# A decoder trunk on one core: state space work and attention probabilities placed otherwise, the gated spatial branch transposed by VectorE and transfers

## The chip, the cores and the metric

The kernel runs on one core of one Trainium2 chip. The metric is the device time of one execution in microseconds (us); several runs are made, and their median counts. A profile of one execution gives the start and the duration of every instruction on the core's engines: TensorE (PE, with its weight loads as PEld), VectorE (DVE), ScalarE (ACT), GpSimd (POOL), and SyncE (SP), whose queue issues nearly all transfers.

## The reference

Two layers, each of three blocks on h, which is 256 tokens by 1024 channels: half a SwiGLU block, a hybrid mixer, half a SwiGLU block, each between a norm before and a norm after. The mixer makes one input projection and sends its columns into three branches:

```python
y_a = moba_attention(q, k, v)            # 8 heads x 128, causal; one block of 256 keys here
xbc = silu(causal_conv(xbc)); dt = softplus(dt_raw + dt_bias)
y_s = ssd_scan(xs, dt, a, bm, cm) + d_skip[:, None] * xs      # 16 heads x 64, chunks of 128
y_s = rms_norm(y_s * silu(z), ssm_norm_g)
u  = gelu(u)
vg = layer_norm(gelu(vg), sgu_ln_g, sgu_ln_b)
sv = einsum('gij,bcjgd->bcigd', tril(sgu_w), vg) + sgu_b      # 8 groups, chunks of 128 tokens
y_c = u * sv
merged = gate0 * (y_a @ p_attn) + gate1 * (y_s @ p_ssm) + gate2 * (y_c @ p_sgu)
out = merged @ w_out
```

All inputs and weights are float32.

## The kernel before

**Tiles.** Tokens stand in two tiles t of 128. A weight block is 128 x 1024 and comes from memory by one transfer (`load`, L160) into a ring of six `raw` tiles. `split` (L180, L181) makes two parts of it, `whi` by ScalarE and `wlo` by VectorE, in rings of eleven. A product takes three matmuls: high by high, low weight by high input, high weight by low input (`unit`, L213 to L215). One call of `unit` is two such triples, six matmuls of 512 columns; a block takes two calls, one for each tile t.

**What sets the order.** Every engine works through its instructions in the order in which the program issues them. The program walks through the matmuls (`gemm`) and after each call of `unit` calls `pump`, which lets `tick` advance the waiting tasks by 1.3 for a call of six matmuls. A task is a generator: what stands between two `yield`s is issued at once, and the number yielded says how long it rests, in units that are near a microsecond of TensorE's work. The table `W` holds these rests. After `tick`, `pump` splits one more weight block, if one was used up. `finish` drives a task to its end at once.

**Layouts.** A product's input is needed with channels on the partitions. Two ways lead there. `to_parts` (L312 and on) transposes 128 x 128 pieces on TensorE into PSUM and makes the high and low part from there. `turn` and `land` go another way: VectorE transposes 32 x 32 squares in place (L277), four transfers write the tile to device memory in another arrangement (L280), and one transfer reads it back (L285); the weights that meet such an input have their rows rearranged on the host (`_woven`). Before the change the SwiGLU hidden tiles, the keys, the probabilities `sc` and the state space result `y` go by `turn`; the spatial branch's `u` goes by `to_parts`.

**The mixer's order.** xbc, z, q, k and v projections with convolution and state space work beside them (`ssd`: for tile t and group g two calls of `weights`, then products `yd`); the first branch product (`br` with `ysh`, `ysl`); projection vg, with attention's tile 1 beside it (`attention`: scores, exponentials, `turn`, `land`, then value products `pv`, L837); the gate and branch product of attention; projection u, with the gelus and the layer norm of vg (`spatial_norm`, L866 to L872); the last gate projection, eight blocks, with the spatial products `sv` (L882, `sgu`) beside it; the last branch product (`br` with `ych`, `ycl`); the output projection.

In `sgu` the tile t = 0 has its two pairs of spatial products, a rest of 9.1 and its transposes; only then comes t = 1. `spatial_norm` issues its work for t = 1 when the u projection has been issued, ahead of `sgu`.

Of the kernel before, what the change touches and what calls it, by code (L numbers as in the profile page):

```python
# [9 lines left out]
F32 = mybir.dt.float32  # L10
BF16 = mybir.dt.bfloat16
F32R = mybir.dt.float32r
AF = mybir.ActivationFunctionType
ALU = mybir.AluOpType
# [30 lines left out]
ACC, TR = 5, 3  # L45


W = {'gw': 6.5, 'tr': 0, 'parts': 0, 'sq': 1.3, 'lead': 3.9, 'sq2': 5.2, 'hh': 5.2, 'x0': 0.65, 'cv': 5.2, 'cs': 6.5, 'xs': 0, 'dt1': 2.6, 'dt2': 0, 'dt3': 5.2, 'cb': 2.6, 'w1': 2.6, 'w2': 6.5, 'ys': 3.9, 'qk': 3.9, 'vv': 0, 'qs': 0, 'ex': 0, 'p1': 10.4, 'p2': 0, 'p3': 3.9, 'ge': 0, 'ln': 10.4, 'sv': 0, 'yc': 9.1, 'mg': 3.9, 'pv': 11.7, 'out': 7.8, 'in': 9.1}


@with_exitstack
def trunk(ctx, tc, a):
# [435 lines left out]
    def mixer(l, x, r2, nxt):  # L488
# [189 lines left out]
        def ssd(ysx, rs):  # L678
# [13 lines left out]
            def scaled(t):  # L692

                y[t] = b4(f"y{t}")
                G.tensor_tensor(h3(y[t]), h3(xs[t]), hpar[:, l, 2, :, None].to_broadcast([P, SH, SP]),
                                op=ALU.mult)
                xdt[t] = xs[t]
                V.tensor_tensor(h3(xdt[t]), h3(xs[t]),
                                st["dt"][:, t * SH:(t + 1) * SH, None].to_broadcast([P, SH, SP]), op=ALU.mult)
# [19 lines left out]
            for t in range(NT):  # L719
                for g in range(SG):  # L720
                    weights(t, 2 * g)
                    if g == 0:
                        scaled(t)
                    yield W["w1"]
                    weights(t, 2 * g + 1)
                    if t == 0:

                        pst = tr("state")
                        T.matmul(pst, bc["b"][:, g * P:(g + 1) * P], xw[:, 512 * g:512 * g + 512],
                                 start=True, stop=True)  # L730
                        A.copy(state[:, 512 * g:512 * g + 512], pst)
                    yield W["w2"]
                    c = slice(512 * g, 512 * g + 512)
                    py = tr("yd")
                    for q in (2 * g, 2 * g + 1):
                        for j in range(4):
                            hh = q * 4 + j
                            T.matmul(py[:, (hh - 8 * g) * SP:(hh - 8 * g + 1) * SP], ws[t, q][:, j, :],
                                     xdt[t][:, hh * SP:(hh + 1) * SP], start=True, stop=True)
                        ws.pop((t, q))  # L740
                    V.tensor_tensor(y[t][:, c], py, y[t][:, c], op=ALU.add)
                    if t == 1:
                        po = tr("yo")
                        T.matmul(po, cT(g, 1), state[:, c], start=True, stop=True)
                        tmp = b2("yo")
                        V.tensor_tensor(h3(tmp, 8), h3(po, 8),
                                        st["eac"][:, 8 * g:8 * g + 8, None].to_broadcast([P, 8, SP]), op=ALU.mult)
                        V.tensor_tensor(y[t][:, c], y[t][:, c], tmp, op=ALU.add)
                    V.tensor_tensor(y[t][:, c], y[t][:, c], zs[t][:, c], op=ALU.mult)
                rs[t] = rsqrt([sumsq(y[t], "sy")], "rs", 1.0 / D)  # L750
                yt[t] = spawn(turned(t, y[t], pl[:, G_SSM:G_SSM + 8]), wait=1.3)


        qk = {}
# [26 lines left out]
        def attention(yax, free):  # L781
            for t in range(NT):
# [36 lines left out]
                for g in range(2):  # L819
# [2 lines left out]
                                    rden[:, None, 4 * g:4 * g + 4, None].to_broadcast([P, 4 * m, 4, 32]), op=ALU.mult)  # L822
                    rd[g] = turn(sc[g], m)
                    yield 1.3
                yield W["out"]
                for g in range(2):
                    land(sc[g].rearrange("p (m e) -> p m e", m=m), rd[g])
                yield W["pv"]
# [13 lines left out]

        uu, vg = {}, {}

        def gelu_evac(store, name, c, ps):

            for t in range(NT):
                if t not in store:
                    store[t] = b4(f"{name}{t}")
                p1 = ps[t]  # L850
                xx = b2("gx")
                A.activation(xx, p1, AF.Copy, scale=r2[t])
                x2 = b2("gx2")
                A.activation(x2, p1, AF.Square, scale=r2[t])
                V.scalar_tensor_tensor(x2, x2, 1.0 / A_GELU, xx, op0=ALU.add, op1=ALU.mult)
                A.activation(x2, x2, AF.Tanh, scale=C_GELU * A_GELU)
                V.scalar_tensor_tensor(store[t][:, 512 * c:512 * c + 512], x2, 1.0, xx, op0=ALU.add, op1=ALU.mult)
                yield W["ge"]

# [15 lines left out]
        def sgu(ycx):  # L875
            ws = wsp[l][0]
            for t in range(NT):
                for q in range(2):
                    ps = tr("sv")
                    for j in range(4):  # L880
                        g = 4 * q + j
                        T.matmul(ps[:, j * P:(j + 1) * P], ws[:, g, :], vg[t][:, g * P:(g + 1) * P],  # L882
                                 start=True, stop=True)
                    for j in range(4):
                        g = 4 * q + j
                        o = uu[t][:, g * P:(g + 1) * P]
                        V.scalar_tensor_tensor(o, ps[:, j * P:(j + 1) * P], pl[:, G_SB + g:G_SB + g + 1], o,
                                               op0=ALU.add, op1=ALU.mult)
                    yield W["sv"]
                yield W["yc"]  # L890
                yield from to_parts(uu[t], *ycx.new(t), scale=0.5)


        merged = {}
# [27 lines left out]
                yield W["mg"]  # L922
                yield from to_parts(merged[t], *then.new(t))

        def branch(bx, rs, need, first=False, then=None):
            store = {}
            es = []
            for c in range(2):
                [ps] = project("gate")
                es.append(spawn(gate_evac(store, c, ps, rs)))  # L930
            finish(*need)
            finish(*es)
            slots, dst = accs("br")
            ready, out = set(), {}

            def on_done(key, t):
                ready.add((key, t))
                if t not in out:
                    out[t] = spawn(merge(t, slots, ready, store, first, then))

            gemm(chunk(0) + chunk(1), bx.h, bx.l, dst, tail=8 if then is not None else 0, on_done=on_done)
            return out

# [27 lines left out]
        b1 = branch(yax, None, [att, *b0.values()])  # L971
        gw = spawn(spatial_weights(l))
        finish(*gl)
        gl = [spawn(gelu_evac(uu, "u", 0, project("u")[0]))]
        finish(gw)
        sn = spawn(spatial_norm())
        gl.append(spawn(gelu_evac(uu, "u", 1, project("u")[0])))
        finish(*gl, sn)
        sg = spawn(sgu(ycx))
        b2_ = branch(ycx, None, [sg, *b1.values()], then=mx)  # L980
        ready = set()

        def mh(k, t):
# [145 lines left out]
def _arrays(i):  # L1129
# [3 lines left out]
    q, k, v, z, xbc, dt, u, vg, g0, g1, g2 = (w[:, :, s:e] for s, e in zip(cut[:-1], cut[1:]))  # L1133
    k = _woven(k, 512)
    weave = lambda m: _woven(np.swapaxes(m, 1, 2), 512).swapaxes(1, 2)
    order = [xbc, z, q, k, v, g1, weave(f["p_ssm"]), vg, g0, f["p_attn"], u, g2, f["p_sgu"], f["w_out"]]
    mix = [_chunks(m).reshape(L, -1, P, 1024) for m in order]
    col = lambda m: m.reshape(L, -1, P).transpose(0, 2, 1)
    par = np.concatenate(
# [39 lines left out]
```

## Time and profile before

| | |
|---|---|
| runs | 1492.39, 1489.04, 1489.55 us; median 1489.55 |
| the profiled execution's own time | 1490.6 us |
| its span, first to last instruction | 1488.8 us |
| mean granted TensorE clock | 0.992 of 2.4 GHz |
| weight blocks | 495, of 512 KB |

TensorE's matmuls overlap: one of 512 columns is shown with 0.39 us, and the next starts 0.23 us after it. An idle time in square brackets ends a row of the timeline, with what ended it. In the windows, PEclk is the granted clock as a share of 2.4 GHz; 0.50 is 1.2 GHz. Times of a layer are those from the span's start; layer 1's mixer comes some 736 us after layer 0's.

### The profile page before, as it was taken

What the parts mean: (1) busy time and instruction counts of PE and PEld (TensorE: products, weight loads), DVE (VectorE), ACT (ScalarE), POOL (GpSimd) and SP (SyncE); (2) the same over time, 40 slices, a digit from 0 to 9 for tenths busy, and PEclk for the clock granted to TensorE, in tenths of its full rate; (3) what the DMA queues carried; (4) which work ended last, traced back from release to release, by engine and by line L of the source; (5) the groups of instructions that cost most, each with busy time, mean ns of one, the idle gap of its engine ahead of it and who ended that gap; (6) DMA issues with size and microseconds to landing.
All of it is one profiled execution on the core that took longest, in us unless ns stands there. A gap on an engine that the chain in (4) does not pass through costs nothing. (4 is left out here: it accounts for less than half of the span.)

```text
span 1488.8 us, 18560 instructions
## 1 busy us (share of the span) xinstructions
PE 1461.8 (98%) x6706; PEld 1208.7 (81%) x6706; DVE 970.3 (65%) x1188; ACT 767.7 (52%) x1051; POOL 55.0 (4%) x98
## 2 busy tenths in 40 slices
PE   9999999989989999999999999999899899999998
PEld 7888888778878888888888888888788788888886
DVE  6766477767666857666486564876776677676652
ACT  6544367455454537444364443765463635464541
POOL 0000020000000000000000000200000000000000
PEclk9999999999999999999999999999999999999999
DMA  8978555577567445878568874656774765477760
GB/s 293 332 228 263 185 191 177 161 209 224 198 213 224 172 156 197 282 243 255 154 205 268 253 251 128 221 171 187 227 230 150 230 211 169 132 261 249 262 199 28
DMA packets 151003, 312.23 MB, mean 210 GB/s; under 512 B 35456, under 2 KB 76544, under 8 KB 150912
## 3 DMA queue, kind: packets, MB, share of 16 engines
q1 hardware_dynamic: 150336, 310.73, 64.3%
q8 instruction: 52, 0.85, 0.2%
q10 hardware_dynamic: 576, 0.33, 0.1%
q14 instruction: 39, 0.32, 0.1%
HBM read 288.98 MB, written 22.02 MB: 209 GB/s over the span
## 5 line engine op out<-in xcount | busy, mean ns | idle before, releaser
L181 DVE TENSOR_TENSOR wlo<-raw,whi 128x1024 fp32r<-128x1024 f32 x495 | 593.9, 1222 | 325.9 <-ACT whi L180 323.5
L180 ACT CAST whi<-raw 128x1024 fp32r<-128x1024 f32 x495 | 511.7, 1051 | 394.8 <-PE gu L215 162.9
L213 PE MATMUL gu<-whi,xh 128*128 128x512 f32 x704 | 276.1, 392 | 1.7 <-ACT xh L328 1.3
L214 PE MATMUL gu<-wlo,xh 128*128 128x512 f32 x704 | 274.9, 391 | 0.0
L215 PE MATMUL gu<-whi,xl 128*128 128x512 f32 x704 | 274.8, 390 | 0.0
L213 PEld LDWEIGHTS gu<-whi,xh 128*128 128x128 f32 x704 | 132.6, 188 | 30.2 <-ACT xh L328 1.7
L214 PEld LDWEIGHTS gu<-wlo,xh 128*128 128x128 f32 x704 | 132.6, 188 | 28.0 <-DVE wlo L169 0.9
L215 PEld LDWEIGHTS gu<-whi,xl 128*128 128x128 f32 x704 | 132.6, 188 | 28.1 <-DVE xl L329 0.4
L213 PE MATMUL dn<-whi,hTh 128*128 128x512 f32 x352 | 137.5, 391 | 0.0
L215 PE MATMUL dn<-whi,hTl 128*128 128x512 f32 x352 | 137.0, 389 | 0.0
L214 PE MATMUL dn<-wlo,hTh 128*128 128x512 f32 x352 | 136.9, 389 | 0.0
L215 PEld LDWEIGHTS dn<-whi,hTl 128*128 128x128 f32 x352 | 66.1, 188 | 13.9
L213 PE MATMUL gate<-whi,xh 128*128 128x512 f32 x192 | 77.1, 402 | 0.0
L214 PEld LDWEIGHTS dn<-wlo,hTh 128*128 128x128 f32 x352 | 66.1, 188 | 13.6
L213 PEld LDWEIGHTS dn<-whi,hTh 128*128 128x128 f32 x352 | 66.1, 188 | 13.3
L215 PE MATMUL gate<-whi,xl 128*128 128x512 f32 x192 | 75.4, 393 | 0.0
L214 PE MATMUL gate<-wlo,xh 128*128 128x512 f32 x192 | 75.2, 392 | 0.0
L328 ACT CAST xh<-xg 128x512 fp32r<-128x512 f32 (+1 forms) x25 | 15.1, 603 | 63.0 <-DVE xg L326 63.0
L713 ACT ACTIVATE ssw<-ssw,nacs 128x128 f32<-128x128 f32 x64 | 20.5, 391 | 50.8 <-DVE ssw L709 50.8
L215 PEld LDWEIGHTS gate<-whi,xl 128*128 128x128 f32 x192 | 36.3, 189 | 7.8
L214 PEld LDWEIGHTS gate<-wlo,xh 128*128 128x128 f32 x192 | 36.4, 190 | 6.9
L213 PEld LDWEIGHTS gate<-whi,xh 128*128 128x128 f32 x192 | 36.4, 190 | 6.8
(239 smaller groups left out, 2231.3 us busy)
## 6 DMA issues: line engine op xcount, KB each, us to landing
raw<-in_mix SPq DMA_DIRECT2D x232, 512.0 KB, 4.5
raw<-in_gu SPq DMA_DIRECT2D x175, 512.0 KB, 4.9
raw<-in_dn SPq DMA_DIRECT2D x88, 512.0 KB, 4.5
turn<-hh SPq DMA_DIRECT2D x160, 64.0 KB, 1.8
hh<-turn SPq DMA_DIRECT2D x40, 256.0 KB, 5.2
row_ffn_post_g<-in_ffn_post_g SPq DMA_DIRECT2D x4, 512.0 KB, 5.7
turnw<-qtok SPq DMA_DIRECT2D x32, 64.0 KB, 2.2
qT<-turnw SPq DMA_DIRECT2D x4, 512.0 KB, 5.9
```

The costliest lines, as they stand in the source:

```text
L180: A.copy(hi, w)
L181: V.tensor_tensor(lo, w, hi.bitcast(F32), op=ALU.subtract)
L213: T.matmul(o, xh(k, t), hi[:, off:off + n], start=first, stop=False)
L214: T.matmul(o, xh(k, t), lo[:, off:off + n], start=False, stop=False)
L215: T.matmul(o, xl(k, t), hi[:, off:off + n], start=False, stop=last)
L328: A.copy(o_h, xg)
L713: A.activation(w[:, j, :], w[:, j, :], AF.Exp, bias=st["nacs"][:, c:c + 1])
```

## The change

Five things change. The scaling of the state space input of tile 1 (`scaled(1)`: one GpSimd and one VectorE operation) is issued with group 1 of tile 0 instead of group 0 of tile 1, and the transposing of y of tile 0 starts after a rest of 6.5 instead of 1.3. The probabilities are read back after a rest of 3.9 instead of 7.8, and the value products follow after 13.0 instead of 11.7. `sgu` issues the spatial products of both tiles one after the other. The gated result u is no longer transposed by TensorE: a new task `turned_sum` for each tile transposes it in place, writes it, reads it back and makes the two parts; the host rearranges the rows of `p_sgu`. The last branch product waits for this task tile by tile (`late`), and the factor 0.5 moves from the transposes into the gelu of u.

```diff
@@ -45,7 +45,7 @@
 ACC, TR = 5, 3
 
 
-W = {'gw': 6.5, 'tr': 0, 'parts': 0, 'sq': 1.3, 'lead': 3.9, 'sq2': 5.2, 'hh': 5.2, 'x0': 0.65, 'cv': 5.2, 'cs': 6.5, 'xs': 0, 'dt1': 2.6, 'dt2': 0, 'dt3': 5.2, 'cb': 2.6, 'w1': 2.6, 'w2': 6.5, 'ys': 3.9, 'qk': 3.9, 'vv': 0, 'qs': 0, 'ex': 0, 'p1': 10.4, 'p2': 0, 'p3': 3.9, 'ge': 0, 'ln': 10.4, 'sv': 0, 'yc': 9.1, 'mg': 3.9, 'pv': 11.7, 'out': 7.8, 'in': 9.1}
+W = {'gw': 6.5, 'tr': 0, 'parts': 0, 'sq': 1.3, 'lead': 3.9, 'sq2': 5.2, 'hh': 5.2, 'x0': 0.65, 'cv': 5.2, 'cs': 6.5, 'xs': 0, 'dt1': 2.6, 'dt2': 0, 'dt3': 5.2, 'cb': 2.6, 'w1': 2.6, 'w2': 6.5, 'ys': 3.9, 'qk': 3.9, 'vv': 0, 'qs': 0, 'ex': 0, 'p1': 10.4, 'p2': 0, 'p3': 3.9, 'ge': 0, 'ln': 10.4, 'sv': 0, 'yc': 9.1, 'mg': 3.9, 'so': 3.9, 'pv': 13.0, 'uo': 5.2, 'out': 7.8, 'in': 9.1}
 
 
 @with_exitstack
@@ -719,8 +719,8 @@
             for t in range(NT):
                 for g in range(SG):
                     weights(t, 2 * g)
-                    if g == 0:
-                        scaled(t)
+                    if t == 0:
+                        scaled(g)
                     yield W["w1"]
                     weights(t, 2 * g + 1)
                     if t == 0:
@@ -748,7 +748,7 @@
                         V.tensor_tensor(y[t][:, c], y[t][:, c], tmp, op=ALU.add)
                     V.tensor_tensor(y[t][:, c], y[t][:, c], zs[t][:, c], op=ALU.mult)
                 rs[t] = rsqrt([sumsq(y[t], "sy")], "rs", 1.0 / D)
-                yt[t] = spawn(turned(t, y[t], pl[:, G_SSM:G_SSM + 8]), wait=1.3)
+                yt[t] = spawn(turned(t, y[t], pl[:, G_SSM:G_SSM + 8]), wait=1.3 if t else 6.5)
 
 
         qk = {}
@@ -822,7 +822,7 @@
                                     rden[:, None, 4 * g:4 * g + 4, None].to_broadcast([P, 4 * m, 4, 32]), op=ALU.mult)
                     rd[g] = turn(sc[g], m)
                     yield 1.3
-                yield W["out"]
+                yield W["so"]
                 for g in range(2):
                     land(sc[g].rearrange("p (m e) -> p m e", m=m), rd[g])
                 yield W["pv"]
@@ -842,18 +842,18 @@
 
         uu, vg = {}, {}
 
-        def gelu_evac(store, name, c, ps):
+        def gelu_evac(store, name, c, ps, half=1):
 
             for t in range(NT):
                 if t not in store:
                     store[t] = b4(f"{name}{t}")
                 p1 = ps[t]
                 xx = b2("gx")
-                A.activation(xx, p1, AF.Copy, scale=r2[t])
+                A.activation(xx, p1, AF.Copy, scale=r2[t] if half == 1 else halfr[t])
                 x2 = b2("gx2")
                 A.activation(x2, p1, AF.Square, scale=r2[t])
                 V.scalar_tensor_tensor(x2, x2, 1.0 / A_GELU, xx, op0=ALU.add, op1=ALU.mult)
-                A.activation(x2, x2, AF.Tanh, scale=C_GELU * A_GELU)
+                A.activation(x2, x2, AF.Tanh, scale=half * C_GELU * A_GELU)
                 V.scalar_tensor_tensor(store[t][:, 512 * c:512 * c + 512], x2, 1.0, xx, op0=ALU.add, op1=ALU.mult)
                 yield W["ge"]
 
@@ -887,8 +887,23 @@
                         V.scalar_tensor_tensor(o, ps[:, j * P:(j + 1) * P], pl[:, G_SB + g:G_SB + g + 1], o,
                                                op0=ALU.add, op1=ALU.mult)
                     yield W["sv"]
-                yield W["yc"]
-                yield from to_parts(uu[t], *ycx.new(t), scale=0.5)
+                yc[t] = spawn(turned_sum(t), wait=1.3)
+
+        yc = {}
+
+        def turned_sum(t):
+            u = uu[t]
+            rd = turn(u, 2)
+            yield W["uo"]
+            land(u.rearrange("p (q e) -> p q e", q=2), rd)
+            yield W["in"]
+            new = ycx.new(t)
+            for q in range(2):
+                o_h, o_l = (x[:, 4 * q:4 * q + 4, :].rearrange("p k (a j) -> p a k j", a=4) for x in new)
+                r4 = u[:, 512 * q:512 * q + 512].rearrange("p (a k j) -> p a k j", a=4, k=4)
+                A.copy(o_h, r4)
+                V.tensor_tensor(o_l, r4, o_h.bitcast(F32), op=ALU.subtract)
+                yield 0.65
 
 
         merged = {}
@@ -922,7 +937,7 @@
                 yield W["mg"]
                 yield from to_parts(merged[t], *then.new(t))
 
-        def branch(bx, rs, need, first=False, then=None):
+        def branch(bx, rs, need, first=False, then=None, late=None):
             store = {}
             es = []
             for c in range(2):
@@ -938,6 +953,8 @@
                 if t not in out:
                     out[t] = spawn(merge(t, slots, ready, store, first, then))
 
+            if late is not None:
+                bx = guarded(bx, gate_on(late, finish))
             gemm(chunk(0) + chunk(1), bx.h, bx.l, dst, tail=8 if then is not None else 0, on_done=on_done)
             return out
 
@@ -971,13 +988,13 @@
         b1 = branch(yax, None, [att, *b0.values()])
         gw = spawn(spatial_weights(l))
         finish(*gl)
-        gl = [spawn(gelu_evac(uu, "u", 0, project("u")[0]))]
+        gl = [spawn(gelu_evac(uu, "u", 0, project("u")[0], 2))]
         finish(gw)
         sn = spawn(spatial_norm())
-        gl.append(spawn(gelu_evac(uu, "u", 1, project("u")[0])))
+        gl.append(spawn(gelu_evac(uu, "u", 1, project("u")[0], 2)))
         finish(*gl, sn)
         sg = spawn(sgu(ycx))
-        b2_ = branch(ycx, None, [sg, *b1.values()], then=mx)
+        b2_ = branch(ycx, None, [sg, *b1.values()], then=mx, late=yc)
         ready = set()
 
         def mh(k, t):
@@ -1133,7 +1150,7 @@
     q, k, v, z, xbc, dt, u, vg, g0, g1, g2 = (w[:, :, s:e] for s, e in zip(cut[:-1], cut[1:]))
     k = _woven(k, 512)
     weave = lambda m: _woven(np.swapaxes(m, 1, 2), 512).swapaxes(1, 2)
-    order = [xbc, z, q, k, v, g1, weave(f["p_ssm"]), vg, g0, f["p_attn"], u, g2, f["p_sgu"], f["w_out"]]
+    order = [xbc, z, q, k, v, g1, weave(f["p_ssm"]), vg, g0, f["p_attn"], u, g2, weave(f["p_sgu"]), f["w_out"]]
     mix = [_chunks(m).reshape(L, -1, P, 1024) for m in order]
     col = lambda m: m.reshape(L, -1, P).transpose(0, 2, 1)
     par = np.concatenate(
```

On TensorE, among the last gate projection's products of layer 0 (`vg_3563` is tile 0, `vg_3578` tile 1; `u_4086` and `u_4112` are the gated tiles 0 and 1), stood before:

```order
L882 MATMUL sv<-vg_3563,wsp 128x128 x4
...
L882 MATMUL sv<-vg_3563,wsp 128x128 x4
...
L312 MATMUL xtr<-con,u_4086 128x128 x4
...
L882 MATMUL sv<-vg_3578,wsp 128x128 x4
...
L882 MATMUL sv<-vg_3578,wsp 128x128 x4
...
L312 MATMUL xtr<-con,u_4112 128x128 x8
L213 MATMUL br<-whi,ych_4327 128x512
```

and stands now:

```order
L882 MATMUL sv<-vg_3563,wsp 128x128 x4
L213 MATMUL gate<-whi,xh_1595 128x512
L214 MATMUL gate<-wlo,xh_1595 128x512
L215 MATMUL gate<-whi,xl_1596 128x512
L213 MATMUL gate<-whi,xh_1595 128x512
L214 MATMUL gate<-wlo,xh_1595 128x512
L215 MATMUL gate<-whi,xl_1596 128x512
L882 MATMUL sv<-vg_3578,wsp 128x128 x4
...
L882 MATMUL sv<-vg_3578,wsp 128x128 x4
```

The first spatial product of tile 1 stood 66 gate matmuls and two groups of transposes behind the second of tile 0; now six gate matmuls are between them, and the transposes of u are gone.

On ScalarE, at the end of the same gate projection (`gate` is the gate's evacuation, `ych` the high part of the branch's input), stood before:

```order
L900 ACTIVATE gate<-gate,halfr 128x512 x2
L180 CAST whi<-raw 128x1024
L321 ACTIVATE ych_4327<-xtr 128x512 x2
L180 CAST whi<-raw 128x1024 x3
L321 ACTIVATE ych_4409<-xtr 128x512 x2
L900 ACTIVATE gate<-gate,halfr 128x512 x2
L180 CAST whi<-raw 128x1024 x3
```

and stands now:

```order
L915 ACTIVATE gate<-gate,halfr 128x512 x2
L180 CAST whi<-raw 128x1024 x4
L915 ACTIVATE gate<-gate,halfr 128x512 x2
L904 CAST ych_4412<-u_4086 128x4x4x32 x2
L904 CAST ych_4436<-u_4112 128x4x4x32 x2
L180 CAST whi<-raw 128x1024 x3
```

Both tiles' high parts moved behind the last weight cast of the gate projection and behind the evacuation of its last gate.

On VectorE, in the state space work of layer 0 (`xs_2189` is the input of tile 1, `y_2468` the result of tile 0, `ssw` the decay weights), stood before:

```order
L709 TENSOR_TENSOR ssw<-seg,con 128x512
L715 TENSOR_TENSOR ssw<-ssw,cbt 128x512
L698 TENSOR_TENSOR xs_2189<-xs_2189,dt 128x1024
L277 STREAM_TRANSPOSE qtok<-qtok 128x512 x2
L277 STREAM_TRANSPOSE y_2468<-y_2468 128x1024
L181 TENSOR_TENSOR wlo<-raw,whi 128x1024
L709 TENSOR_TENSOR ssw<-seg,con 128x512
L715 TENSOR_TENSOR ssw<-ssw,cbt 128x512
L181 TENSOR_TENSOR wlo<-raw,whi 128x1024 x3
```

and stands now:

```order
L709 TENSOR_TENSOR ssw<-seg,con 128x512
L715 TENSOR_TENSOR ssw<-ssw,cbt 128x512
L277 STREAM_TRANSPOSE qtok<-qtok 128x512 x2
L181 TENSOR_TENSOR wlo<-raw,whi 128x1024
L709 TENSOR_TENSOR ssw<-seg,con 128x512
L715 TENSOR_TENSOR ssw<-ssw,cbt 128x512
L181 TENSOR_TENSOR wlo<-raw,whi 128x1024 x2
L277 STREAM_TRANSPOSE y_2468<-y_2468 128x1024
L181 TENSOR_TENSOR wlo<-raw,whi 128x1024
```

The scaling of `xs_2189` went ten rows forward, into the stage before, and the transposing of `y_2468` four rows back, behind the last decay weights of this stage.

## Rows read from the trace of the kernel before

**Rows 1.** The page, busy time of each engine over the span.
```profile
PE 1461.8 (98%) x6706; PEld 1208.7 (81%) x6706; DVE 970.3 (65%) x1188; ACT 767.7 (52%) x1051; POOL 55.0 (4%) x98
```

**Rows 2.** Waits of TensorE: engine, line, releaser, us in total, times, longest.
```profile
PE pv L837 <- DMA sc<-turn: 9.1, 2, 4.6
PE yd L738 <- DVE ssw L715: 7.7, 2, 3.8
```

**Rows 3.** Timeline of PE, layer 0, transposes of u: start, duration, line, tiles.
```profile
508.80 0.39 PE L215 MATMUL gate<-whi,xl 128*128 128x512 f32 x1
509.03 0.60 PE L312 MATMUL xtr<-con,u 128*128 128x128 f32 x4
509.38 0.48 PE L213 MATMUL gate<-whi,xh 128*128 128x512 f32 x1
509.70 0.40 PE L214 MATMUL gate<-wlo,xh 128*128 128x512 f32 x1
```

**Rows 4.** Timeline of PE, layer 0, spatial products among the gate products.
```profile
493.61 1.05 PE L882 MATMUL sv<-vg,wsp 128*128 128x128 f32 x8
...
495.88 1.05 PE L882 MATMUL sv<-vg,wsp 128*128 128x128 f32 x8
...
498.14 0.39 PE L213 MATMUL gate<-whi,xh 128*128 128x512 f32 x1
```

**Rows 5.** Timeline of DVE, layer 0: layer norm of tile 1, gating of tile 0.
```profile
505.54 1.28 DVE L872 SCALAR_TENSOR_TENSOR vg<-vg,rv,row_sgu_ln_b 128x1024 f32<-128x1024 f32 x1 [0.71 <-POOL rv L264]
506.74 2.15 DVE L887 SCALAR_TENSOR_TENSOR u<-sv,par,u 128x128 f32<-128x128 f32 x8
```

**Rows 6.** Timeline of PE, layer 1: the second pair of spatial products.
```profile
1231.47 1.05 PE L882 MATMUL sv<-vg,wsp 128*128 128x128 f32 x8
```

**Rows 7.** Timeline of DVE, layer 1: layer norm of tile 1.
```profile
1241.14 1.28 DVE L872 SCALAR_TENSOR_TENSOR vg<-vg,rv,row_sgu_ln_b 128x1024 f32<-128x1024 f32 x1 [0.72 <-POOL rv L264]
```

**Rows 8.** Timeline of PE, both layers: value products, with the idle time before.
```profile
432.60 3.75 PE L837 MATMUL pv<-sc,v 128*128 128x128 f32 x16 [4.42 <-DMA sc<-turn]
...
1169.66 3.44 PE L837 MATMUL pv<-sc,v 128*128 128x128 f32 x16 [4.65 <-DMA sc<-turn]
```

**Rows 9.** Windows of 1 us: length, busy per engine, PEclk, DMA share, GB/s.
```profile
438.00:439.00 1.00, 1.00 (x6) 0.81 (x5) 0.00 (x0) 0.13 (x1) 0.00 (x0) 0.62 0.95 381
...
1172.00:1173.00 1.00, 1.00 (x8) 1.00 (x8) 1.00 (x1) 0.00 (x0) 0.00 (x0) 0.68 0.91 348
```

**Rows 10.** Timeline of ACT, layer 0, around the end of the gate products.
```profile
519.22 1.05 ACT L180 CAST whi<-raw 128x1024 fp32r<-128x1024 f32 x1 [3.00 <-PE gate L215]
520.17 1.08 ACT L321 ACTIVATE ych<-xtr 128x512 fp32r<-128x512 f32 x2
521.14 1.27 ACT L900 ACTIVATE gate<-gate,halfr 128x512 f32<-128x512 f32 x2
```

**Rows 11.** Timeline of PE, layer 0: state space product after its wait.
```profile
318.54 1.30 PE L738 MATMUL yd<-xs,ssw 128*128 128x64 f32 x8 [3.83 <-DVE ssw L715]
```

**Rows 12.** Timeline of DVE, layer 0: the two operations that the change moves.
```profile
311.19 1.21 DVE L698 TENSOR_TENSOR xs<-xs,dt 128x1024 f32<-128x1024 f32 x1
...
313.54 1.20 DVE L277 STREAM_TRANSPOSE y<-y 128x1024 f32<-128x1024 f32 x1
```

**Rows 13.** Timeline of PE, layer 0: first branch product of tile 1, third matmul.
```profile
368.35 0.39 PE L215 MATMUL br<-whi,ysl 128*128 128x512 f32 x1
```

**Rows 14.** Timeline of DVE, layer 0: low part of y, tile 1.
```profile
367.44 0.69 DVE L675 TENSOR_TENSOR ysl<-y,ysh 128x512 fp32r<-128x512 f32 x1 [0.69 <-ACT ysh L674]
```

**Rows 15.** Timeline of SP's DMA queue, layer 0: probabilities of tile 1 read back.
```profile
418.34 7.77 SPq L160 DMA_DIRECT2D raw<-in_mix  x4
426.22 0.93 SPq L285 DMA_DIRECT2D sc<-turn  x2
```

**Rows 16.** DMA issues: transfer, engine, count, KB each, median us to landing.
```profile
turn<-y SPq DMA_DIRECT2D x16, 128.0 KB, 2.6
y<-turn SPq DMA_DIRECT2D x4, 512.0 KB, 6.4
```


## Prediction

> **What bounds the kernel now.** I read the page first: TensorE is busy 98% of the span, VectorE 65%, ScalarE 52% [rows 1]. So the end moves with TensorE alone: with what it has to do, with what it waits for, and with its clock. The list of its waits comes next. It is short: 9.1 us for probabilities that are read back, 7.7 us for the decay weights of the state space work, one of each in either layer [rows 2]. All else must be read from the timeline, engine by engine, around the places where the change puts instructions: first TensorE there, then the engine that feeds it. The reader is to see two things. A wait that TensorE does not have today can be covered by nothing more than a distance in its queue, and the change removes such a distance. And half of what the change aims at is a chain on VectorE that TensorE meets again a little later.
>
> **The spatial products of tile 1.** In layer 0 the second pair of products of tile 0 starts at 495.88, six gate matmuls follow, and the next matmul starts at 498.14 [rows 4]. That is now the place of the first product of tile 1. It needs the layer norm of tile 1, whose last operation starts at 505.54 and takes 1.28, so it ends at 506.82 [rows 5]. TensorE's products stand in one queue: behind this one are 78 gate matmuls and the other spatial product, and for them wait the evacuation of the gates and the weight casts that need freed blocks. The wait is 506.82 - 498.14 = 8.7 us. Before, 66 gate matmuls at 0.23 us, 15 us, stood there and covered it. The VectorE operations ahead of 505.54 keep their order and their inputs, which come from the u projection; nothing in the change makes them start earlier against TensorE. Layer 1 repeats it: 1231.47 + 2.26 = 1233.73 for the place [rows 6], 1241.14 + 1.28 = 1242.42 for the norm [rows 7], again 8.7. Together **+17.4**.
>
> **The clock behind it.** After the idle times of 4.42 and 4.65 us [rows 8] TensorE worked at 0.50, 1.2 GHz. The windows in which 2.4 GHz came back show means of 0.62 and 0.68 [rows 9], so it came back at 438.76 and 1172.64, after 6.2 and 3.0 us of work; half of that was lost, 3.1 and 1.5 us. An idle time of 8.7 is longer than either, so I expect the fall, and take 2.3 for each layer: **+4.6**, bounds 3.0 and 6.2.
>
> **The start of the last branch product.** In ScalarE's queue the high part `ych` now stands behind the last weight cast and the evacuation of the last gate, and both of these wait for the last gate matmul. From its end: 1.05 for the cast, 1.27 for the two evacuations, 0.54 for the first of two `ych` operations [rows 10], 0.1 for the hand-over: 3.0 us. A matmul that follows directly starts 0.16 before the end of the one ahead; the third matmul needs `ycl` from VectorE, some 0.1 more. That is 3.2 a layer, **+6.4**. TensorE has nothing else queued here: the branch product of tile 1 stands behind that of tile 0. Before, tile 0's parts were made in the middle of the gate projection. For the clock I take 0.7 a layer, between nothing and the 1.5 seen after longer idle times: **+1.4**.
>
> Whether the data are there by then: TensorE resumes at 506.9 at half clock and ends the last spatial product by 513; gating half a tile takes 1.1 [rows 5], the transposing in place 1.2 [rows 12]. The four writes land 2.6 after issue, the read-back 6.4 after its own [rows 16]; with two weight loads between them in SP's queue that is about 527.5. The gate projection ends at 506.9 + 78 x 0.23 + 1.8 + 2.3 = 529, and ScalarE turns to `ych` 2.3 later. So the transfers have some 4 us to spare, and only because of the first wait. VectorE's four extra transposings, 4.8 us, lie where TensorE waits or has work, and cost nothing more; if that cover were gone, they would be late by that much at most.
>
> **The transposes.** Four transposes of u hold TensorE from 509.03 to 509.38, and the matmul behind them is followed 0.32 later instead of 0.23 [rows 3]: 0.44 for four, eight such groups go: **-3.5**. The neighbours that read from PSUM are replaced by as many from the tile itself.
> A rule speaks against this part. The Trainium skill, "VectorE: DVE Perf Modes", section "Rules for kernel authors", advises TensorE for 128 x 128 transposing when the result may be in PSUM, as it may here. The row above bears the rule out in delay: 0.44 us for four pieces against 1.2 us on VectorE, four writes and a read-back for eight. By the rule this term would be no gain at all and the sum 3.5 higher; I keep the -3.5, since these are the rows of the engine that sets the end.
>
> **State space.** TensorE waited 3.83 us at 318.54 [rows 11]. Ahead of that wait VectorE did the scaling, 1.21, and the transposing of y, 1.20 [rows 12], both of which now stand elsewhere; at the wait itself some 2.5 us go, and half-clock work behind it with them. But VectorE's chain runs on without a break into the parts of y of tile 1, and there TensorE has almost no room: the low part ends at 367.44 + 0.69 = 368.13 [rows 14], the matmul that reads it starts at 368.35 [rows 13]. Only the scaling left this chain for good, the transposing is in it as before. So TensorE keeps about 1.2 + 0.2 = 1.4 in layer 0. In layer 1 I allow a little more; I take 2 a layer, **-4.0**. Bounds: nothing, and -12, which is both waits and their clock. The scaling costs some 0.4 at most in the stage where it now stands.
>
> **Probabilities.** The value products of tile 1 come 18 matmuls, 4.1 us, earlier in TensorE's queue. Their data do not come that much earlier: the read-back went out at 426.22 behind four weight loads [rows 15] and now goes behind two, and each load waits for a weight split on VectorE of about 1.2; so it goes out 2.3 earlier and has two loads less ahead of it. The wait of 4.42 changes by 4.1 - 2.3 - 1.2 = 0.6 a layer: **+1.2**. Bounds: -8, the waits gone, and +3.6, no help from the missing loads.
>
> **The sum** is 17.4 + 4.6 + 6.4 + 1.4 - 3.5 - 4.0 + 1.2 = 23.5 us. The profiled execution took 1490.6, so 1514.1; it lies 1.05 above the median of the runs, 1489.55, and against that I predict **1513 us**. With the terms at their nearer bounds this case reaches from 1503 to 1522.
>
> **Rivals.**
> 1. *The read-back comes late.* The tiles' transfers wait in SP's queue behind weight loads, and those behind VectorE. If `ych` comes 6 us a layer after its place instead of 4 us before, the sum is 12 higher: **1525**. For it: 6.4 us is a median among other traffic. Against: 10 us is a long way to miss. Chance 0.14.
> 2. *The chain is freed for good.* The state space wait goes with its clock (-9 in place of -4), the value products no longer wait long (-2 in place of +1.2), `ych` costs 2 a layer without a fall of the clock (4.0 in place of 7.8), and the clock after 8.7 us comes back soon (3.0): 17.4 + 3.0 + 4.0 - 3.5 - 9 - 2 = 10: **1499**. For it: the waits themselves are these lengths. Against: rows 13 and 14. Chance 0.09.
> 3. *Faster.* The layer norm of tile 1 is done when TensorE comes to it. VectorE would have to be 8.7 us ahead of where it stands today; then neither of the new waits nor their clock would be there, and -3.5 - 4.0 + 1.2 = -6.3 is left: **1483**. It decides at the first spatial product of tile 1: below a wait of some 2 us there the kernel is no slower. For it: VectorE idles in short pieces of 0.7 us inside this chain [rows 5]. Against: these are hand-overs to other engines, which the change leaves, and nothing is taken from the chain. Chance 0.05.
>
> **How the numbers follow.** My forecast has 0.72. The range is 1500 to 1525: it holds the forecast's own 1503 to 1522, about half of rival 1 and part of rival 2. A difference of 0.2%, 3 us, is about what a measurement of this kernel can tell from no change. Slower by more: the forecast and rivals 1 and 2 but for a small rest, 0.91. Faster: rival 3 but for a rest, 0.05. Within 0.2%: those rests, 0.04.
>
> **What would show it.** In the waits of TensorE a new one of the spatial products for the layer norm, twice, 8 to 9 us; a new one of `br` for `ych` or `ycl`, twice, about 3; the wait of `yd` down from 3.83 to about 1; waits of `br` for `ysh` or `ysl` of some 1.5; the wait of `pv` between 4 and 6; stretches at 0.50 behind the long ones. The forecast is wrong if the spatial products of tile 1 wait less than 5 us, or if `br` waits for the read-back and not for ScalarE's queue.

## The result and the profile after

The changed kernel takes **1515.2 us** (median of 4 runs, 1514.55 to 1517.37) against 1489.78 for the kernel before, run beside it (4 runs). The ratio is 1.017, 95% interval 1.0158 to 1.0182: 25.4 us slower. 1513 was predicted, with a range of 1500 to 1525. The profiled execution took 1517.37, with a span of 1515.6; it is the longest of the four, and all rows below come from it.

The page of the changed kernel, busy time of each engine; it answers to [rows 1]:

```profile
PE 1465.9 (97%) x6674; PEld 1209.7 (80%) x6674; DVE 976.4 (64%) x1192; ACT 768.2 (51%) x1051; POOL 57.0 (4%) x98
```

TensorE has 32 matmuls less, the transposes of u, and is busy 4.1 us longer. Fewer instructions with more busy time mean that some of them ran at the lower clock. The rest of the loss is idle time. The list of TensorE's waits, answering to [rows 2] (releaser, us in total, times, longest):

```profile
PE sv L882 <- DVE vg L872: 17.3, 2, 8.7
PE pv L837 <- DMA sc<-turn: 8.0, 2, 4.1
PE br L213 <- ACT ych L904: 5.7, 2, 2.9
PE yd L738 <- DVE ssw L715: 4.6, 4, 1.4
PE br L213 <- ACT ysh L674: 3.1, 2, 1.6
```

The first and the third line are new, once in each layer: 23.0 us together. `yd` fell from 7.7 to 4.6, but it now waits four times and `br` waits 3.1 for `ysh`: those two make 7.7 again. `pv` fell by 1.1.

TensorE's timeline around the new waits (start, duration, tiles, and in brackets the idle time and its end); the first three rows answer to [rows 4], the fourth to [rows 6], the last two to the branch product of either layer:

```profile
496.51 1.05 PE L882 MATMUL sv<-vg,wsp 128*128 128x128 f32 x8
...
498.55 0.39 PE L215 MATMUL gate<-whi,xl 128*128 128x512 f32 x1
507.61 2.05 PE L882 MATMUL sv<-vg,wsp 128*128 128x128 f32 x8 [8.67 <-DVE vg L872]
...
1255.30 2.04 PE L882 MATMUL sv<-vg,wsp 128*128 128x128 f32 x8 [8.67 <-DVE vg L872]
...
532.62 0.50 PE L213 MATMUL br<-whi,ych 128*128 128x512 f32 x1 [2.85 <-ACT ych L904]
...
1280.22 0.50 PE L213 MATMUL br<-whi,ych 128*128 128x512 f32 x1 [2.85 <-ACT ych L904]
```

The eight spatial matmuls take 1.05 us before the wait and 2.05 behind it: half the clock. On VectorE, the norm that the wait names, answering to [rows 5]:

```profile
506.18 1.28 DVE L872 SCALAR_TENSOR_TENSOR vg<-vg,rv,row_sgu_ln_b 128x1024 f32<-128x1024 f32 x1 [0.72 <-POOL rv L264]
```

It is 0.64 later than before, as is the first spatial product (494.25 now). Nothing in VectorE's chain moved against TensorE. ScalarE's queue at the end of the gate projection, answering to [rows 10]:

```profile
529.85 1.04 ACT L180 CAST whi<-raw 128x1024 fp32r<-128x1024 f32 x1 [1.71 <-DMA raw<-in_mix]
530.80 1.26 ACT L915 ACTIVATE gate<-gate,halfr 128x512 f32<-128x512 f32 x2
531.96 2.17 ACT L904 CAST ych<-u 128x512 fp32r<-128x512 f32 x4
```

`ych` follows the gate's evacuation without a gap, and no wait for the read-back is named: the 2.85 us are ScalarE's queue. The read-back of tile 0 had gone out at 522.10 on SP's queue, and one of u takes 6.7 us in the median here (6.4 for y before, [rows 16]). By this estimate it landed near 528.8, some 3 us before `ych` took its turn.

The stretches of 1 us in which the clock fell and came back (length, busy time of each engine, granted clock, DMA share, GB/s), with a longer one for `br` in layer 1:

```profile
512.00:513.00 1.00, 1.00 (x7) 0.98 (x6) 0.00 (x0) 0.74 (x1) 0.00 (x0) 0.65 0.78 246
533.00:534.00 1.00, 1.00 (x4) 0.56 (x3) 1.00 (x3) 1.00 (x3) 0.00 (x0) 0.59 1.01 127
536.00:537.00 1.00, 1.00 (x4) 0.76 (x3) 0.00 (x0) 0.00 (x0) 0.00 (x0) 0.71 0.02 8
1260.00:1261.00 1.00, 1.00 (x9) 1.00 (x9) 0.00 (x0) 0.98 (x1) 0.00 (x0) 0.89 0.82 315
1280.00:1285.00 5.00, 4.78 (x13) 3.55 (x14) 2.50 (x4) 1.73 (x4) 0.00 (x0) 0.66 0.43 134
```

A mean of 0.65 means 2.4 GHz again at 512.70, 5.1 us after TensorE resumed; in layer 1 it came back at 1260.22, after 4.9. Half of that is lost: 5.0 us for both layers. Behind the wait for `ych` TensorE starts at full clock (0.50 for the first matmul; where it starts at half clock, as in e10_nonorm1, that one takes 0.79), falls at 533.2 and is back at 536.6; 3.4 us at half clock, and as much in layer 1 (a mean of 0.66 over 5 us): 3.4 us lost in all.

### The profile page after: what moved, and what is told of

Read it like the earlier page. It is cut to its first block, busy times and chain, and to the rows that moved or that the text cites. A ratio compares the mean times of both kernels' runs of the same rounds, so it can differ in the third digit from the quotient of the medians.

```text
span 1515.6 us, 18530 instructions
## 1 busy us (share of the span) xinstructions
PE 1465.9 (97%) x6674; PEld 1209.7 (80%) x6674; DVE 976.4 (64%) x1192; ACT 768.2 (51%) x1051; POOL 57.0 (4%) x98
## 5 line engine op out<-in xcount | busy, mean ns | idle before, releaser
L214 PEld LDWEIGHTS dn<-wlo,hTh 128*128 128x128 f32 x352 | 66.1, 188 | 13.6
L215 PEld LDWEIGHTS dn<-whi,hTl 128*128 128x128 f32 x352 | 66.1, 188 | 13.6
```

Source lines behind the costliest of these rows:

```text
L214: T.matmul(o, xh(k, t), lo[:, off:off + n], start=False, stop=False)
L215: T.matmul(o, xl(k, t), hi[:, off:off + n], start=False, stop=last)
```

## Experiments

Ten kernels ran. Times are medians, and ratios those to the kernel before on the same chip. Of an edit only the words that change are shown; `...` stands for what is left out.

| run | what it is | us | ratio, 95% interval |
|---|---|---|---|
| e1_ssd | before + state space part | 1490.16 | 0.9998 (0.9989 to 1.0007) |
| e2_pv | before + probabilities part | 1489.06 | 0.9986 (0.9978 to 0.9995) |
| e3_sgu | changed kernel without these two | 1518.74 | 1.0186 (1.0172 to 1.0200) |
| e4_order | before + order of spatial products | 1512.82 | 1.0146 (1.0132 to 1.0160) |
| e5_rest | changed + rest between the tiles | 1504.14 | 1.0098 (1.0083 to 1.0113) |
| e6_norm0 | changed, tile 1 reads tile 0's norm | 1510.74 | 1.0139 (1.0109 to 1.0169) |
| e7_early | changed, parts made earlier | 1509.08 | 1.0129 (1.0114 to 1.0144) |
| e8_later | before, value products later | 1476.75 | 0.9912 (0.9897 to 0.9927) |
| e9_nosv1 | changed, no products of tile 1 | 1508.89 | 1.0128 (1.0111 to 1.0145) |
| e10_nonorm1 | changed, no norm of tile 1 | 1496.39 | 1.0049 (1.0033 to 1.0065) |

### The three parts of the change, each alone

**e1_ssd**, the kernel before with the state space edits:

```
-                    if g == 0:
-                        scaled(t)
+                    if t == 0:
+                        scaled(g)
...
-  wait=1.3)
+  wait=1.3 if t else 6.5)
```

> The kernel before with the state space part of the change alone (the scaling of tile 1 one stage earlier, the transposing of y of tile 0 later). Theory A, from the two traces: TensorE's wait at the decay weights falls from 3.8 us to 1.4, but VectorE's chain is hardly shorter, so TensorE meets it again at the first branch product of tile 1 (a wait for ysh of about 1.5) and at the second group (0.9): 1491 us, between +2 and 0 against before, with the loss in layer 0. Theory B, that of my prediction: 2 us a layer stay, 1486. Theory C, the chain is freed: 1480 or below.

No gain that can be measured. The waits of TensorE in e1_ssd show why:

```profile
PE pv L837 <- DMA sc<-turn: 9.6, 2, 5.3
PE yd L738 <- DVE ssw L715: 4.6, 4, 1.4
PE br L213 <- ACT ysh L674: 3.1, 2, 1.6
```

The 3.1 us that `yd` gave up are the 3.1 us of `br`. VectorE comes no sooner to the parts of y of tile 1, and TensorE meets it there; the rows are in the part on the prediction.

**e2_pv**, the kernel before with the probabilities' edits:

```
-'pv': 11.7
+'so': 3.9, 'pv': 13.0
...
-                yield W["out"]
+                yield W["so"]
                 for g in range(2):
                     land(sc[g]
```

> The kernel before with the probabilities' part alone (read back after 3.9, value products after 13.0). Theory A, from the two traces: the wait of the value products stays near 4.1 and the clock behind it comes back at about the same moment, a gain of 1 to 2.5 us in all: 1488. Theory B, that of my prediction: the value products come too early for their data and wait 0.6 a layer more: 1491. Theory C, the wait goes: 1482 or below.

About 2 us faster (0.9986). In layer 0 the read-back still ends the wait, in layer 1 it is another one:

```profile
PE pv L837 <- DVE vg L857: 4.4, 1, 4.4
PE pv L837 <- DMA sc<-turn: 3.9, 1, 3.9
```

SP's queue and TensorE in layer 0 of e2_pv; the rows before are [rows 15] and [rows 8]:

```profile
423.02 0.93 SPq L285 DMA_DIRECT2D sc<-turn  x2
...
427.46 3.37 PE L837 MATMUL pv<-sc,v 128*128 128x128 f32 x16 [3.86 <-DMA sc<-turn]
```

From the read-back's issue to the products it is 4.4 us; before it was 6.4.

**e3_sgu**, the changed kernel with both of these undone, so that only the spatial part is left:

```
-                    if t == 0:
-                        scaled(g)
+                    if g == 0:
+                        scaled(t)
...
-'so': 3.9, 'pv': 13.0
+'so': 7.8, 'pv': 11.7
```

> The changed kernel with the state space part and the probabilities' part undone: the spatial branch's part alone. Theory A: the whole loss is here, a wait of 8.7 for the layer norm and of 2.9 for ych in either layer, the clock behind both, less 3.5 for the transposes: 1515 to 1517. Theory B: a good part of the loss comes from the other two parts or from all three together: 1508 or below.

1518.74 is above the 1515 to 1517 expected. The whole loss lies in the spatial part, 28 us, and the other two take some 2.4 us off it, by the ratios (1.0186 here, 1.0170 for the changed kernel).

### Order or transfers

**e4_order** keeps TensorE's transposes and moves only the products, so that those of both tiles stand one after the other:

```
                     yield W["sv"]
+            for t in range(NT):
                 yield W["yc"]
                 yield from to_parts(uu[t], *ycx.new(t), scale=0.5)
```

> The kernel before with one thing of the spatial part: both tiles' spatial products are issued one after the other, and the transposes of u stay on TensorE, each tile's after the rest of 9.1. No transfers of u. Theory A: the order of the products alone brings the wait of 8.7 and its clock in either layer (17.4 + 5), and with tile 0's parts made in the middle of the gate projection there is no wait for ych: 1512. Theory B, the transfers and their place in the queues make the loss: 1490 to 1495.

1512.82, 22 us above before: the order alone costs about what the first wait and its clock take in the changed kernel, 17.3 + 5.0 (the clock took 5.9 in e4_order's own profile). Its list of waits has the same `sv` line and none of `br`; it begins:

```profile
PE sv L882 <- DVE vg L872: 17.3, 2, 8.7
PE pv L837 <- DMA sc<-turn: 9.0, 2, 4.6
```

From e4_order to e3_sgu it is 5.9 us more, the price of the transfers in place of TensorE's transposes: 5.7 of waiting for `ych` and 3.4 of clock, which leaves -3.2 for the transposes saved. No run measures these by themselves, and the -3.2 holds whatever else differs between the two runs.

**e7_early** shortens the rest ahead of the parts in `turned_sum` from 9.1, so that `ych` stands earlier in ScalarE's queue:

```
-            yield W["in"]
+            yield 5.2
```

> The changed kernel with the parts of u issued three calls earlier (a rest of 5.2 instead of 9.1 behind the read-back), so that ych stands ahead of the last weight casts and of the last gate's evacuation in ScalarE's queue. Theory A: in the trace of the changed kernel the read-back of tile 0 lands near 529 and the gate projection ends near 530, so the wait of br falls from 2.9 to 1 or less and its clock stays up: 6 to 9 us less than the changed kernel, 1507. Theory B: the wait belongs to the read-back and not to the queue: no gain, 1515.

1509.08, 6 us less than the changed kernel, and no wait of `br` for `ych` is left:

```profile
PE sv L882 <- DVE vg L872: 17.4, 2, 8.7
...
PE br L213 <- ACT ysh L674: 3.1, 2, 1.6
```

So this wait was a place in ScalarE's queue and not the transfers. But there is no more to be had from that place, as ScalarE shows in e7_early:

```profile
526.51 0.62 ACT L904 CAST ych<-u 128x512 fp32r<-128x512 f32 x1 [3.67 <-DMA u<-turn]
```

Here ScalarE waits for the read-back, and TensorE's first `br` matmul starts at 527.18, as soon as this cast allows. The gain is below the 9.1 of wait and clock. In part that is the clock elsewhere: in the state space work and the first branch product it took 5.1 us in this profile (both in layer 1) and 3.4 in the changed kernel's (both in layer 0).

**e5_rest** sets a rest between the two tiles in `sgu`, as far as stood there before, and keeps the transfers:

```
                 yc[t] = spawn(turned_sum(t), wait=1.3)
+                if t == 0:
+                    yield 14.3
```

> The changed kernel with one rest put back: between the spatial products of tile 0 and those of tile 1 the task rests 14.3, so that TensorE has 72 gate matmuls there again. The transfers of u stay. Theory A: the wait of 8.7 and its clock go, but now the gate projection ends at its old time and u of tile 0 is read back some 4 us later than that: br waits about 5 a layer, for the read-back and no longer for ScalarE's queue alone, with its clock; 1498, still slower than before. Theory B: the order of the products was the whole loss, and the transfers are hidden: 1486 or below.

1504.14, 6 above the 1498 expected. The wait of `sv` is gone; in its place stand, in TensorE's list:

```profile
PE br L213 <- ACT ych L906: 10.3, 2, 5.2
...
PE br L215 <- DVE ycl L907: 3.3, 2, 1.7
```

ScalarE says what `ych` waited for:

```profile
518.19 1.26 ACT L917 ACTIVATE gate<-gate,halfr 128x512 f32<-128x512 f32 x2
521.14 1.14 ACT L906 CAST ych<-u 128x512 fp32r<-128x512 f32 x2 [1.69 <-DMA u<-turn]
```

This time the read-back comes last, 1.69 us behind ScalarE's queue, which makes up most of the rest of the 5.2. Without the first wait the transfers are no longer covered: `br` waits 13.6 us in all, where the changed kernel waited 17.3 for the norm and 5.7 for `ych`.

### What makes the spatial products wait

**e6_norm0** lets the spatial products of tile 1 read tile 0's norm; the norm of tile 1 still runs, and is left out of the result:

```
-  ws[:, g, :], vg[t][:, g * P:(g + 1) * P]
+  ws[:, g, :], vg[0][:, g * P:(g + 1) * P]
```

> The changed kernel in its own order, but the spatial products of tile 1 read the layer norm of tile 0 (so tile 1's spatial branch is not the reference's). TensorE need not wait for the norm of tile 1, and all else stays in its place. Theory A: the wait of 8.7 goes and most of it comes back at br, since gating and the transfers of u come behind the norm on VectorE: a wait of 7 to 9 for the read-back and a loss of clock behind it; 1504 to 1508. Theory B, my rival of a faster kernel: without that wait nothing is late, 1483 to 1490.

It missed: the median is 1510.74, and though two of the four runs took 1507.9, the upper end of what was expected (the others 1513.5 and 1515.8, at a lower mean clock), the wait did not go. It moved to the next group of products and shrank by 1.3 only. TensorE's timeline of e6_norm0, which ends in the middle of the last row's eight matmuls:

```profile
496.34 1.05 PE L882 MATMUL sv<-vg,wsp 128*128 128x128 f32 x8
...
498.38 0.39 PE L215 MATMUL gate<-whi,xl 128*128 128x512 f32 x1
506.12 1.22 PE L882 MATMUL sv<-vg,wsp 128*128 128x128 f32 x4 [7.36 <-DVE u L887]
```

and VectorE's:

```profile
503.75 1.28 DVE L872 SCALAR_TENSOR_TENSOR vg<-vg,rv,row_sgu_ln_b 128x1024 f32<-128x1024 f32 x1 [0.72 <-POOL rv L264]
504.95 2.15 DVE L887 SCALAR_TENSOR_TENSOR u<-sv,par,u 128x128 f32<-128x128 f32 x8
```

The first group of tile 1 runs now. The second, the fourth since the start, waits for the gating of tile 0, which frees a PSUM buffer and stands behind the norm of tile 1 in VectorE's queue. So two locks hung on one queue, and I had named one.

**e10_nonorm1** is e6_norm0 and leaves out the norm of tile 1 altogether (in `spatial_norm`):

```
-            for t in range(NT):
+            for t in range(1):
```

> The changed kernel without the layer norm of tile 1: its spatial products read the normed tile 0. Theory A, in the kernel whose products of tile 1 read tile 0's norm the fourth pair still waited for a PSUM buffer that the gating of tile 0 frees, and this stands behind the norm of tile 1 in VectorE's queue: without that norm the wait of sv goes from 7.4 to some 2.7 us a layer, br waits 3 to 5 us for ych, about 1500 us (1496 to 1504). Rival, the 7.4 us are not a matter of VectorE's queue (the gating is late for another reason): the wait stays above 6 us and the time at about 1511.

1496.39, within what was expected and 6 above the kernel before, and the wait is as expected (TensorE's timeline of e10_nonorm1):

```profile
502.73 1.16 PE L882 MATMUL sv<-vg,wsp 128*128 128x128 f32 x8 [2.59 <-DVE u L887]
```

The wait of the changed kernel is thus VectorE's place in its chain: 8.67 with norm and gating, 7.36 with the gating alone behind the norm, 2.59 with the gating alone. What is left is the GELU of tile 1, which stands ahead of the gating and ends at 501.64, and the four gating operations behind it. The clock held here: the eight matmuls take 1.16, and the granted clock is 1.00 in every window of 5 us from 495 to 510.

**e9_nosv1** leaves out the spatial products of tile 1, whose gating reads those of tile 0:

```
-                    ps = tr("sv")
...
+                    if t == 0:
+                        pss[q] = tr("sv")
...
+                    ps = pss[q]
```

> The changed kernel without the spatial products of tile 1: its gating reads the products of tile 0, so 16 products a layer, 1.6 us of TensorE, are left out, and TensorE can wait here neither for the norm nor for a PSUM buffer. Theory A, the read-back was covered only by the first wait: that wait and its clock go (-17.3 - 5.0 - 3.2 for the work left out), but br now waits for u read back, some 7 us a layer in place of 2.9: about 1498 us (1494 to 1503). Rival: the transfers have room of their own and br waits 2.9 as in the changed kernel: about 1490.

The direction is right, the size is not: 1508.89. `br` waits 11.46 in place of some 7 (TensorE's and then ScalarE's timeline of e9_nosv1):

```profile
514.75 0.39 PE L215 MATMUL gate<-whi,xl 128*128 128x512 f32 x1
526.60 0.79 PE L213 MATMUL br<-whi,ych 128*128 128x512 f32 x1 [11.46 <-ACT ych L907]
```

```profile
519.07 1.04 ACT L180 CAST whi<-raw 128x1024 fp32r<-128x1024 f32 x1 [5.28 <-DMA raw<-in_mix]
520.02 1.26 ACT L918 ACTIVATE gate<-gate,halfr 128x512 f32<-128x512 f32 x2
525.93 1.14 ACT L907 CAST ych<-u 128x512 fp32r<-128x512 f32 x2 [4.65 <-DMA u<-turn]
```

TensorE is done with the gates at 515, the read-back comes at 525.9. The gating of tile 0 still stands behind the norm, so the transposes, four writes and a read-back start no sooner than VectorE allows. The weight cast ahead of the gate's evacuation is late too: it waits for a block whose load went out at 514.38, behind the writes of u in SP's queue. Though TensorE has neither the norm nor the PSUM buffer to wait for, the kernel is still 19 us slower than before: what the first wait no longer costs, the transfers take.

### A faster one

**e8_later** is e2_pv with one number changed:

```
-'so': 3.9, 'pv': 13.0
+'so': 3.9, 'pv': 20.8
```

The value products of tile 1 stand further back in TensorE's queue, the read-back as early as in e2_pv.

> The kernel before with the probabilities read back after 3.9 and the value products after 20.8, that is with the change's early read-back, but the value products later than before instead of earlier. Theory A: the data land near 430.5 in layer 0 and TensorE comes near 431.6, so the wait of 9 us and the clock behind it, some 4, go: 1478, faster than both kernels. Theory B: the transfers are as late as TensorE is, or the parts of the attention's result come too late for their branch product: 1487 or above.

1476.75, 0.9912 of before: 13 us faster than the kernel before and some 38 faster than the changed one. The waits of `pv` are gone, and the clock with them. Windows of 5 us, e8_later:

```profile
430.00:435.00 5.00, 5.00 (x32) 4.43 (x31) 4.56 (x5) 5.00 (x7) 0.00 (x0) 1.00 0.87 333
435.00:440.00 5.00, 5.00 (x32) 4.42 (x31) 4.53 (x6) 4.02 (x6) 0.00 (x0) 1.00 0.91 297
```

and the kernel before:

```profile
430.00:435.00 5.00, 2.40 (x11) 2.44 (x12) 4.06 (x5) 4.40 (x5) 0.00 (x0) 0.69 1.01 342
435.00:440.00 5.00, 5.00 (x25) 4.42 (x24) 1.98 (x3) 1.75 (x3) 0.00 (x0) 0.62 0.95 365
```

It is the changed kernel's mistake turned round: more distance in TensorE's queue ahead of data that come late.

## Why the prediction was right, term by term

The mechanism was right: the order of the spatial products makes most of the loss, at the place and of the size that the prediction gave. The sum was 23.5, and 25.4 were measured between medians.

| term | predicted | measured | from |
|---|---|---|---|
| wait of `sv` | +17.4 | +17.3 | list of waits |
| clock behind it | +4.6 | +5.0 | windows |
| wait for `ych` | +6.4 | +5.7 | list of waits |
| clock behind that | +1.4 | +3.4 | windows |
| transposes | -3.5 | about -3.2 | what is left of e3_sgu less e4_order, less the two rows above |
| state space | -4.0 | -0.3 (-1.6 to +1.0) | ratio of e1_ssd |
| probabilities | +1.2 | -2.1 (-3.3 to -0.7) | ratio of e2_pv |

The measured terms make 25.8; as the transposes' term is a remainder, this is no proof of each. The first two were read from rows at their own place, and e4_order confirms them together. Three others were off.

**State space, -4.0.** The step that failed is "TensorE keeps about 1.2 + 0.2 = 1.4 in layer 0". In e1_ssd TensorE gains 2.4 us at the first group (from 3.83 to 1.43) and gives it back: 0.89 at the second group, for which the sum had no wait, and 1.58 at `ysh`. The step took the chain to be shorter by the scaling. It is not: the low part of tile 1 starts at 367.68 in e1_ssd and at 367.44 before [rows 14]. VectorE's timeline of e1_ssd:

```profile
340.72 1.25 DVE L277 STREAM_TRANSPOSE y<-y 128x1024 f32<-128x1024 f32 x1 [1.30 <-ACT junk L270]
...
367.68 0.69 DVE L675 TENSOR_TENSOR ysl<-y,ysh 128x512 fp32r<-128x512 f32 x1 [0.68 <-ACT ysh L674]
```

The transposing of y of tile 1 now waits 1.30 us for ScalarE's sum of squares. Before, VectorE made the parts of tile 0 in that time; with the later transposing of tile 0 these have moved behind it. Nor does the chain run on "without a break", as the prediction has it. In the kernel before VectorE waits for a weight cast that stands behind the exponentials in ScalarE's queue:

```profile
357.86 1.23 DVE L181 TENSOR_TENSOR wlo<-raw,whi 128x1024 fp32r<-128x1024 f32 x1 [4.20 <-ACT whi L180]
```

The measured value is inside the noted bounds, at the end of nothing gained.

**Probabilities, +1.2.** The step "the wait of 4.42 changes by 4.1 - 2.3 - 1.2 = 0.6 a layer" is wrong in sign: the waits are 4.09 and 3.93 in the changed kernel, against 4.42 and 4.65 [rows 8]. In layer 0 of e2_pv the wait fell by 0.56. TensorE came 4.2 earlier to it, as forecast; but the read-back went out 2.8 earlier against TensorE's work where 2.3 were allowed, and took 1.9 less from issue to use where the missing loads were given 1.2.

**The clock behind `ych`, +1.4.** 0.7 a layer was taken between nothing and 1.5; it was 1.7 a layer, more than the range said. That is no fixed price. The same wait of 2.85 us stands in both layers of three other kernels. The clock took 1.7 behind each in e3_sgu, nothing and then 3.1 in e6_norm0, 3.1 and then nothing in e10_nonorm1. Windows behind it in e6_norm0, layer 0 and layer 1:

```profile
528.00:533.00 5.00, 4.78 (x20) 3.64 (x21) 2.50 (x4) 1.74 (x4) 0.00 (x0) 1.00 0.44 139
...
1275.00:1280.00 5.00, 4.71 (x11) 3.71 (x12) 2.50 (x4) 1.79 (x4) 0.00 (x0) 0.50 0.42 134
```

State space came out 3.7 slower than forecast and the probabilities 3.3 faster, so the total is near the forecast partly by luck.

The prediction said that the transfers had 4 us to spare "and only because of the first wait". It was some 3 against ScalarE's queue, and e5_rest and e9_nosv1 show the second half. Rival 1, the late read-back, was therefore wrong here and right as soon as the first wait is taken away. Rival 2 falls with e1_ssd, where the waits of TensorE are as long as before. Rival 3 had the right place but one condition too few. It asked for the norm alone; e6_norm0 shows that the gating of tile 0 and its PSUM buffer (there are three of its kind, `TR = 3`) must come in time too. In e9_nosv1, where TensorE waits for neither but VectorE is no earlier, the kernel is 19 us slower than before; in e10_nonorm1, with the norm gone from VectorE, 6. What a VectorE that is 8.7 us ahead would give, the rival's own condition, no run shows.

## What to carry to other kernels

In a queue that is worked off in order, distance is the cover of a wait: before products are moved together, subtract the time of their inputs from the place where they will stand, and look also at the buffers that they need and at who frees them. A wait that a busy engine's chain makes moves to the next place where the chain is met, unless work leaves the chain. A transfer in place of an engine's work is free only while something else covers its whole length, from the last input to the first use (from the transposing in place to `ych` 12.4 us in e5_rest, 14.8 in e9_nosv1). The same search for distance gave e8_later its 13 us.

## What the runs showed that was not expected

The granted clock after short waits differs from layer to layer, as behind `ych` above. The wait of `yd` for the first decay weights is 1.43 or 1.44 us in both layers of the following kernels, and the 8 us in which it ends or that follow it have a mean of 1.00, 0.79 or 0.57. In e1_ssd, layer 0 and layer 1:

```profile
316.00:324.00 8.00, 7.08 (x32) 5.39 (x33) 7.10 (x9) 3.65 (x5) 0.00 (x0) 1.00 0.84 258
...
1052.00:1060.00 8.00, 7.76 (x29) 5.93 (x30) 6.22 (x8) 3.51 (x5) 0.00 (x0) 0.79 0.86 260
```

and in layer 1 of e7_early, whose layer 0 has 1.00:

```profile
1060.00:1068.00 8.00, 8.00 (x24) 5.99 (x25) 5.22 (x5) 3.23 (x5) 0.00 (x0) 0.57 0.89 273
```

A mean of 0.57 over 8 us is 3.4 us lost, one of 0.79 is 1.7. The Trainium skill, "TensorE: Matmul & The Clock Gate", section "What's actually happening", says that the number of slow matmuls at a start varies between runs of one kernel; here the variation is behind waits in the middle of a kernel, and a change of a few us, as in e1_ssd, can't be read from a single profile because of it. What decides it was not found out.
